# The samples' attention: own-maximum exponentials and value sums on VectorE, with shares and norm in small steps

## The chip, the core and the metric

One core of a Trainium2 chip runs the whole program. Its engines are TensorE (PE in the profile: matrix products, with PEld for the loading of the stationary operand), VectorE (DVE), ScalarE (ACT), GpSimd (POOL) and SyncE (SP), which issues most DMAs; each engine works through its own queue in order, and semaphores hold an instruction until its inputs are there. TensorE writes its results to PSUM (8 banks here, four in the pool `pmm` and four in `paux`), which DVE and ACT read; POOL does not touch PSUM in this kernel. The metric is the device time of one execution in microseconds, lower is better; the median of several runs is compared.

## The reference

One inference step of two layers, for a prompt of 256 tokens and for 8 samples of one token each, which share the weights. Each layer: a half-weighted SwiGLU, a mixer (a short gated convolution in layer 0, a gated linear recurrence in layer 1), cross attention to 256 memory rows, a second SwiGLU; a norm ahead of each. All is float32, and x has 1024 columns. The part that the change touches is the cross attention:

```python
def cross_attn(x, mk, mv, w_q, w_o):
    B, T, D = x.shape
    q = (x @ w_q).reshape(B, T, X_HEADS, X_HEAD_DIM)
    s = jnp.einsum('bthd,bnhd->bhtn', q, mk.astype(q.dtype)).astype(jnp.float32) / math.sqrt(X_HEAD_DIM)
    p = jax.nn.softmax(s, axis=-1).astype(x.dtype)
    o = jnp.einsum('bhtn,bnhd->bthd', p, mv.astype(x.dtype)).reshape(B, T, D)
    return o @ w_o
```

The prompt's keys and values (`mk`, `mv`) are products of the memory with `w_xkv`, made here; the 8 samples have keys and values of their own, read from a cache of 256 rows, 4 heads and 256 columns per sample and layer.

## The kernel before

**Layout.** x is held transposed (`xT`: 8 blocks of 128 columns of the model, each 264 wide: 256 prompt tokens and 8 samples), so each product serves prompt and samples at once. float32 products are made of three: each factor is split into a high part rounded to the fast product format and the rest (`xh`, `xl` of x; `wh`, `wl` of a weight), and `mm3` (L336 to L338) multiplies high x high, high x low, low x high.

**Weights** (class `Weights`). They come in halves of 4 blocks (512 KB) through six raw buffers, loaded on SP's queue (L96), rounded to `wh` on ACT (L107) and split to `wl` on DVE or POOL, as `W.lo` says (L122: "v" or "p"). `advance()` does one split, one rounding and the loads that fit, once per `flow.tick()`; a half can be rounded once a buffer out of five is free (`first_live` marks the first half still in use). `W.after` names an instruction behind which later roundings or splits on an engine have to stand, and `order(a, b)` puts a behind b in an engine's queue.

**Flow.** Work beside the main products is written as generators in three lanes; each `flow.tick()` between products advances every lane by one step up to its next `yield`. A planner then orders each engine's queue: by and large in the order of issue, but an instruction whose inputs it takes to be ready can run ahead of its step; `tc.high_priority(offset=HURRY)` moves some forward.

**Norms** (class `Norm`). For each block of x that is finished, `high`, `low` and `square` make `xh` (ACT), `xl` (DVE, L361) and add the square to `acc` (ACT, then POOL, L373). After the last block, `finish` waits three steps, splits `acc` (`nhi` on ACT, `nlo` on DVE, L383), and one step later makes the factor R from a product with ones, Ln and Exp on ACT and three dependent DVE steps (L324 to L330). The next projection runs on unscaled x meanwhile; R is first needed when its results leave PSUM (`evac_q`, L952, for the queries).

**Attention of one layer** (`attention`). `project` makes the queries of the four heads (tile `qT`), two heads first side by side in 8 steps. In lane 1 `mem_split` makes `mh` (ACT, L943) and `ml` (DVE, L944) of the memory. `do_kv(h)` makes keys and values of the prompt for one head: 8 blocks of 6 products of 512 columns (L966 to L968, tile `kv`), with a tick after each; then lane 1 follows with `transpose_k` (`pkt`, `KTt`), `prompt_scores` (`psc`, softmax, `ppt`) and `prompt_values` (`po`, into `oh` and `ol`). `project_late` is the output projection: it runs over blocks 0 to 5 for three chunks (two first, then the third) before the last head of the prompt is complete, and then ends.

**The samples** run in lane 0. `sample_scores(h)` lays each sample's query on 16 partitions and multiplies and adds with 16 key rows per partition on DVE (L1020, two instructions a row), four rows per step; partition 16b+g holds rows of sample b. After all four heads `sample_rest` takes the maximum over heads and partitions through two small products (`pst`), the exponentials for all heads, a third small product for the sums, multiplies shares into `Ps` (L1108, one column per sample) and makes 64 products of 8 rows and 256 columns with the value rows (L1122, tile `spv`, four heads beside each other in the array), four value rows of all heads per step, then a copy, two transposes (`spt`), and the last 8 columns of `oh` and `ol`. Key and value rows come through `Ring`: four buffers of 1 MB, filled on SP's queue in the order of the line (8 of keys, 8 of values per layer, then the state tiles for the recurrence), each as soon as `ring.done` gives a buffer back. `W.lo` is "p" from the end of `project` until the samples are drained, just ahead of `project_late`.

## Time and profile before

| | |
|---|---|
| median of 3 runs | 1293.19 us (1293.01 to 1293.26) |
| the profiled execution | 1294.13 us |
| its span, first to last instruction | 1292.3 us |
| mean granted TensorE clock | 0.998 |
| HBM read / written | 259.19 MB / 10.10 MB |

The profile is of one execution. Its page gives each engine's busy time, 40 slices of the span, the DMA queues, the chain of work that ended last, and the costliest groups of instructions; the trace also answers by stretch of time, by tile, by line and by wait. "core: us, PE busy (x) ..." rows give, per stretch, length, busy time and count of each engine, the granted clock, the mean share of the 16 DMA engines that was busy, and the rate in GB/s. In rows of groups, out<-in is followed by the shapes, the count, then busy us and mean ns of one, then idle time ahead of it and who ended it. In rows in order of time, the first number is the start and the second the length, in us; brackets hold idle time and its releaser. A matmul's listed duration is its passage through the array; several are under way at once.

### The profile page before, as it was taken

The page shows a single profiled execution, that of the slowest core. Times are in us where ns is not written, and L with a number is a line of the kernel's source. Part 1 is how long each engine was busy: PE and PEld are TensorE (multiplying, and loading weights), DVE is VectorE, ACT ScalarE, POOL GpSimd, SP SyncE. Part 2 cuts the span into 40 slices and gives each one's busy share as a digit, 9 for nine tenths or more (in the row PEclk, how much of TensorE's full clock was granted, in tenths as well). Part 3 has the DMA queues.
Part 4 walks back from the last instruction along what each step waited for, and adds up shares of the span by engine and source line. Part 5 has one row for each costly group of instructions (what it writes and reads, how often), then busy time and mean ns, then how long its engine had stood idle before and what let it go on. Part 6 is the DMA issues. An engine that isn't in the chain of part 4 may idle for free.

```text
span 1292.3 us, 25856 instructions
## 1 busy us (share of the span) xinstructions
PE 1271.4 (98%) x10267; PEld 1233.7 (95%) x10267; DVE 826.4 (64%) x1561; ACT 692.4 (54%) x1131; POOL 292.1 (23%) x236
## 2 busy tenths in 40 slices
PE   8999999999999999999999999999999999999996
PEld 8999999999869999999999999999998789999996
DVE  7655567759925755546655545887888728766454
ACT  6455545446545655544645544656575446766542
POOL 2211231212650211132111132000013531112220
PEclk9999999999999999999999999999999999999999
DMA  8796555646998666556666656563547995997550
GB/s 274 239 304 178 167 180 183 197 148 196 352 372 255 185 176 191 172 165 193 191 181 179 183 168 193 175 189 114 189 149 238 393 359 151 292 315 236 167 164 35
DMA packets 263755, 270.98 MB, mean 210 GB/s; under 512 B 8777, under 2 KB 259721, under 8 KB 261074
## 3 DMA queue, kind: packets, MB, share of 16 engines
q1 hardware_dynamic: 257726, 263.98, 64.9%
q10 hardware_dynamic: 5908, 5.35, 1.2%
q8 instruction: 81, 1.33, 0.4%
q14 instruction: 40, 0.33, 0.1%
HBM read 259.19 MB, written 10.10 MB: 208 GB/s over the span
## 4 chain that ended last, share of the span: by engine, by line
PE 92%; DVE 4%; ACT 1%; issue 1%; DMA 1%; POOL 0%; SPq 0%; DVEq 0%; ACTq 0%; POOLq 0%
PE pj L336 19%; PE pj L337 19%; PE pj L338 19%; PE dn L336 7%; PE dn L338 7%; PE dn L337 7%; PE kv L967 2%; PE kv L966 2%; PE kv L968 2%; DVE xl L361 2%; DVE wl L122 1%; PE spv L1122 1%; PE psc L1048 1%; PE pj L414 1%; PE pl L1288 1%
## 5 line engine op out<-in xcount | busy, mean ns | idle before, releaser
L122 DVE TENSOR_TENSOR wl<-raw,wh 128x1024 fp32r<-128x1024 f32 (+1 forms) x348 | 426.7, 1232 | 240.4 <-ACT wh L107 228.1
L336 PE MATMUL pj<-xh,wh 128*128 128x264 f32 x1952 | 558.4, 286 | 5.0 <-DVE qT L952 2.5
L337 PE MATMUL pj<-xl,wh 128*128 128x264 f32 x1952 | 553.4, 284 | 0.0
L338 PE MATMUL pj<-xh,wl 128*128 128x264 f32 x1952 | 553.0, 283 | 0.0
L107 ACT CAST wh<-raw 128x1024 fp32r<-128x1024 f32 (+1 forms) x406 | 415.9, 1032 | 255.5 <-PE pj L337 121.5
L336 PEld LDWEIGHTS pj<-xh,wh 128*128 128x128 f32 x1952 | 367.8, 188 | 7.3 <-DVE qT L952 3.0
L337 PEld LDWEIGHTS pj<-xl,wh 128*128 128x128 f32 x1952 | 368.0, 189 | 0.0
L338 PEld LDWEIGHTS pj<-xh,wl 128*128 128x128 f32 x1952 | 366.2, 188 | 0.0
L336 PE MATMUL dn<-ah,wh 128*128 128x264 f32 x704 | 200.9, 285 | 0.0
L338 PE MATMUL dn<-ah,wl 128*128 128x264 f32 x704 | 200.0, 284 | 0.0
L337 PE MATMUL dn<-al,wh 128*128 128x264 f32 x704 | 199.4, 283 | 0.0
L816 POOL TENSOR_TENSOR al<-a,ah 128x264 fp32r<-128x264 f32 x88 | 90.4, 1029 | 411.8 <-ACT ah L815 411.6
L122 POOL TENSOR_TENSOR wl<-raw,wh 128x1024 fp32r<-128x1024 f32 (+1 forms) x60 | 140.5, 2351 | 186.1 <-ACT wh L107 119.9
L338 PEld LDWEIGHTS dn<-ah,wl 128*128 128x128 f32 x704 | 132.7, 188 | 0.0
L336 PEld LDWEIGHTS dn<-ah,wh 128*128 128x128 f32 x704 | 132.4, 188 | 0.2
L337 PEld LDWEIGHTS dn<-al,wh 128*128 128x128 f32 x704 | 132.5, 188 | 0.0
L312 ACT ACTIVATE g<-g 128x264 f32<-128x264 f32 x88 | 36.9, 424 | 76.3 <-DVE g L808 76.3
L815 ACT CAST ah<-a 128x264 fp32r<-128x264 f32 x88 | 36.0, 413 | 69.0 <-DVE a L814 68.9
L356 ACT ACTIVATE xh<-xT,gains 128x264 fp32r<-128x264 f32 x56 | 28.2, 513 | 74.2 <-DVE xT L842 59.1
L1020 DVE CUSTOM_DVE_ANT_0 junk<-ring,pq 128x256 f32<-128x256 f32 x128 | 53.7, 419 | 3.7
L808 DVE TENSOR_TENSOR g<-pj,R_norm_ffn 128x264 f32<-128x264 f32 x88 | 37.5, 430 | 28.5 <-PE pj L338 28.2
L814 DVE TENSOR_TENSOR a<-g,pj 128x264 f32<-128x264 f32 x88 | 37.1, 426 | 26.2 <-PE pj L338 25.2
(325 smaller groups left out, 1481.3 us busy)
## 6 DMA issues: line engine op xcount, KB each, us to landing
raw<-in_w_ffn_gate_dram SPq DMA_DIRECT2D x88, 512.0 KB, 5.6
raw<-in_w_ffn_up_dram SPq DMA_DIRECT2D x88, 512.0 KB, 3.8
raw<-in_w_ffn_down_dram SPq DMA_DIRECT2D x64, 512.0 KB, 3.4
ring<-in_cache_mem_k_dram SPq DMA_DIRECT2D x16, 1024.0 KB, 7.7
raw<-in_w_xkv_dram SPq DMA_DIRECT2D x64, 256.0 KB, 4.8
ring<-in_cache_mem_v_dram SPq DMA_DIRECT2D x16, 1024.0 KB, 8.7
raw<-in_w_rec_in_dram SPq DMA_DIRECT2D x32, 512.0 KB, 4.2
raw<-in_w_ffn_down_dram SPq DMA_DIRECT2D x32, 384.0 KB, 2.9
```

What stands on the lines that cost most here:

```text
L107: ins = self.behind(self.hi[i % len(self.hi)], copy(wh[:, :n], self.raw[i][:, :n]))
L122: ins = eng.tensor_sub(wl[:, :n], self.raw.pop(i)[:, :n], wh[:, :n].bitcast(F32))
L312: in_line(nc.scalar.activation(dst, src, func, **kw))
L336: nc.tensor.matmul(ps, wh[:, s], rh, start=first, stop=False)
L337: nc.tensor.matmul(ps, wh[:, s], rl, start=False, stop=False)
L338: nc.tensor.matmul(ps, wl[:, s], rh, start=False, stop=last)
L356: W.pin(nc.scalar.activation(xh[:, k, :n], src, AF.Copy, scale=gcol(self.name, self.layer, k)))
L808: nc.vector.tensor_mul(g, ps, norm.R)
L814: nc.vector.tensor_mul(a, g, ps)
L815: nc.scalar.copy(ah[:, blk], a)
L816: nc.gpsimd.tensor_sub(al[:, blk], a, ah[:, blk].bitcast(F32))
L1020: nc.vector.tensor_tensor_reduce(junk, t[:, i % 8], pq[:, :XD], 1.0, 0.0, ALU.mult, ALU.add, sc[:, h, i : i + 1])
```

## The change

Per layer, the diff does this:

- `sample_scores`: five key rows per step instead of four; when a head's 16 scores are there, each partition takes its own negative maximum and its own exponentials and their sum. The queries leave PSUM already divided by 16.
- `sample_rest`: after five idle steps, DVE sums the value rows for a pair of heads at a time, weighted with the unscaled exponentials: 16 rows x 2 heads, two rows per step, in a PSUM bank (`acc`); the last row goes to `total` in SBUF. Between the rows of the first pair, `combine` makes, one small piece per step, the common maximum, the correction factor of each partition, the common sum, and `oz`: the share factor, laid out per sample. Per pair, four products of `total` with `oz` (8 columns) then give the samples' output already transposed. The maxima, corrections and products are ordered behind the big product issued last (`flow.passed`).
- The value rows come as four rows of two heads per buffer, no longer two rows of four heads.
- Nothing drains the samples ahead of the output projection. `project_late` needs the first pair before block 0 and the second before block 4, and goes over blocks 0 to 3 of all three chunks before it goes to blocks 4 and 5.
- DVE to other engines: the memory's low part (`ml`) and the prompt's `vl` go to POOL (with one more copy on ACT for `ml`), the keys' copy `KTt` and the softmax's scaling go to ACT. `W.lo` is "p" from the seventh step of `mem_split` until the second pair is done.
- `Norm.finish`: ahead of the attention (`early`) the split of `acc` comes one step earlier, and in the step before the factor no weights are split or rounded (`held`); for the norm behind the attention, `xl` of the last four blocks is made behind the split of `acc`.

```diff
+SLACK = 5
+STEPS = (3, 5, 7, 9, 11, 13)
+LAG = 2
...
 
     def advance(self):
         n = len(self.halves)
-        if self.n_split < self.n_round:
+        if not self.held and self.n_split < self.n_round:
             self._split()
-        if self.n_round < n and self.n_round - self.first_live < W_BUFS:
+        if not self.held and self.n_round < n and self.n_round - self.first_live < W_BUFS:
             self._round()
...
         def finish(self):
-            yield
-            yield
-            yield
+            for _ in range(3 - self.early):
+                yield
             hi, lo = (cp.tile([P, NC], F32R, tag="nsq", name=n, bufs=2) for n in ("nhi", "nlo"))
-            nc.scalar.copy(hi, self.acc)
-            nc.vector.tensor_sub(lo, self.acc, hi.bitcast(F32))
-            yield
+            into = nc.scalar.copy(hi, self.acc)
+            rest = nc.vector.tensor_sub(lo, self.acc, hi.bitcast(F32))
+            if self.early or self.lows:
+                W.after["s"], W.after["v"] = into.ins, rest.ins
+            for k in self.lows:
+                W.behind("v", self.low(k))
+            for n in range(1 + self.early):
+                W.held = self.early and n == 1
+                yield
+            W.held = False
             ps = aux_bank("ps_ms")
...
+        for a, b in ((0, HK), (HK, k0)):
+            need(a)
+            for k in range(a, b):
+                for c in range(2):
+                    block(c, k)
+                if k == HK - 1:
+                    W.first_live = first[0] + 2
                 flow.tick()
+            for k in range(a, b):
+                block(2, k)
+                if k == HK - 1:
+                    W.first_live = first[1]
+                if k % 2:
+                    flow.tick()
         ready()
...
-        def fill_v(i2):
+        def fill_v(pair, i4):
             def f(t):
                 rows = ins["cache_mem_v"][l].rearrange("b (g i) h d -> (b g) i (h d)", i=NI)
-                nc.sync.dma_start(t.rearrange("p (i e) -> p i e", i=2), rows[:, 2 * i2 : 2 * i2 + 2])
+                at = slice(2 * pair * XD, 2 * pair * XD + 2 * XD)
+                nc.sync.dma_start(t.rearrange("p (i e) -> p i e", i=4), rows[:, 4 * i4 : 4 * i4 + 4, at])
 
             return f
...
+        if late is not None:
+            nxt.lows = range(KT - 4, KT)
...
+                    nxt.low(k - 1)
+            nxt.kt(k, low=k != KT - 2 if late is None else k not in nxt.lows)
...
                     yield
+                W.lo = ("p",)
                 for k in range(KT):
                     g = gcol("norm_mem", l, k)
-                    nc.scalar.activation(mh[:, k], memT[:, k], AF.Copy, scale=g)
-                    nc.vector.scalar_tensor_tensor(
-                        ml[:, k], memT[:, k], g, mh[:, k].bitcast(F32), op0=ALU.mult, op1=ALU.subtract
-                    )
+                    mg = ap.tile([P, NMEM], F32, tag="mg", name=f"mg{k}", bufs=2)
+                    W.behind("s", nc.scalar.activation(mg, memT[:, k], AF.Copy, scale=g))
+                    nc.scalar.copy(mh[:, k], mg)
+                    nc.gpsimd.tensor_sub(ml[:, k], mg, mh[:, k].bitcast(F32))
                     yield
 
-                nc.vector.tensor_mul(qTs[h][:, j], ps, norm.R)
+                nc.vector.scalar_tensor_tensor(qTs[h][:, j], ps, 1.0 / 16.0, norm.R, op0=ALU.mult, op1=ALU.mult)
...
-                nc.vector.tensor_sub(vl, vn, vh.bitcast(F32))
+                nc.gpsimd.tensor_sub(vl, vn, vh.bitcast(F32))
...
-                nc.vector.tensor_copy(KTt[h], pt.rearrange("p (t n) -> p t n", t=2))
+                nc.scalar.copy(KTt[h], pt.rearrange("p (t n) -> p t n", t=2))
...
-                    if i % 4 == 3:
+                    if i % 5 == 4:
                         yield
+                nc.vector.reduce_max(mx[:, h : h + 1], sc[:, h], axis=AX.X, negate=True)
+                act(sc[:, h], sc[:, h], AF.Exp, bias=mx[:, h : h + 1], accum_out=zs[:, h : h + 1])
...
-                    nc.vector.tensor_scalar(pr[:, r], pr[:, r], zs[:, r : r + 1], None, op0=ALU.mult)
+                    nc.scalar.activation(pr[:, r], pr[:, r], AF.Copy, scale=zs[:, r : r + 1])
...
+            def combine():
+                pt = aux_bank("pst")
+                order(nc.tensor.transpose(pt[:XH, :P], mx, ident), flow.passed, "products in line")
+                yield
+                top, f, g = pt[:XH, 2 * P : 2 * P + NB], pt[:, P + 2 * XH : P + 3 * XH], pt[:, P + 3 * XH : P + 4 * XH]
+                nc.vector.tensor_reduce(top, pt[:XH, :P].rearrange("h (b g) -> h b g", b=NB), axis=AX.X, op=ALU.min)
+                nc.vector.tensor_copy(tops[:XH].rearrange("h (b g) -> h b g", b=NB), spread(top))
+                yield
+                order(
+                    nc.tensor.matmul(pt[:, P : P + XH], tops, ident[:, :XH], start=True, stop=True),
+                    flow.passed,
+                    "products in line",
+                )
+                nc.vector.tensor_sub(mx, pt[:, P : P + XH], mx)
+                act(f, mx, AF.Exp)
+                yield
+                nc.vector.tensor_mul(zs, zs, f)
+                yield
+                order(
+                    nc.tensor.matmul(pt[:, P + XH : P + 2 * XH], peers, zs, start=True, stop=True),
+                    flow.passed,
+                    "products in line",
+                )
+                yield
+                nc.vector.reciprocal(rz, pt[:, P + XH : P + 2 * XH])
+                nc.vector.tensor_mul(g, rz, f)
+                nc.vector.tensor_mul(
+                    oz, g.unsqueeze(2).broadcast_to([P, XH, NB]), own.unsqueeze(1).broadcast_to([P, XH, NB])
+                )
             def sample_rest():
...
+                for _ in range(SLACK):
+                    yield
+                steps = combine()
+                for pair in range(XH // 2):
+                    acc = aux_bank("acc")
+                    total = ap.tile([P, 2, XD], F32, tag="total", name="total", bufs=1)
+                    for i in range(NI):
+                        t = ring.tiles[l, "v", pair, i // 4].rearrange("p (i h d) -> p i h d", i=4, h=2)
+                        for j in range(2):
+                            p, sums = sc[:, 2 * pair + j, i : i + 1], acc[:, j * XD : j * XD + XD]
+                            if i == 0:
+                                nc.vector.tensor_scalar(sums, t[:, i % 4, j], p, None, op0=ALU.mult)
+                            else:
+                                dst = total[:, j] if i == NI - 1 else sums
+                                nc.vector.scalar_tensor_tensor(
+                                    dst, t[:, i % 4, j], p, sums, op0=ALU.mult, op1=ALU.add
+                                )
+                        if i % 4 == 3:
+                            ring.done((l, "v", pair, i // 4))
+                        if pair == 0 and i in STEPS:
+                            next(steps, None)
+                        if i % 2:
+                            yield
+                    for _ in range(LAG):
+                        yield
+                    pt = aux_bank("spt")
+                    for j in range(2):
+                        for dt in range(2):
+                            o = pt[:, (2 * j + dt) * NB : (2 * j + dt) * NB + NB]
+                            d = slice(dt * P, dt * P + P)
+                            order(
+                                nc.tensor.matmul(o, total[:, j, d], oz[:, 2 * pair + j], start=True, stop=True),
+                                flow.passed,
+                                "products in line",
                             )
+                    with tc.high_priority(offset=HURRY):
+                        ptv = pt[:, : 4 * NB].rearrange("p (t b) -> p t b", b=NB)
+                        ohv, olv = (t[:, 4 * pair : 4 * pair + 4, T:] for t in (oh, ol))
+                        nc.scalar.copy(ohv, ptv)
+                        nc.vector.tensor_sub(olv, ptv, ohv.bitcast(F32))
+                    sampled.add(pair)
                     yield
+
+            def until(pair):
+                while pair not in sampled:
+                    flow.step()
+                if pair:
+                    W.lo = ("v",)
 
             flow.spawn(1, mem_split())
             project(XH, xh, xl, evac_q, need=norm)
-            W.lo = ("p",)
             for h in range(XH):
                 do_kv(h)
-            flow.drain(0)
-            W.lo = ("v",)
-            out_proj(oh, ol, nxt, late=(KT - 2, lambda: flow.drain(1)))
+            out_proj(oh, ol, nxt, late=(KT - 2, lambda k: until(k // 4), lambda: flow.drain(1)))
```

`mm3` now returns its last product, which `flow.passed` keeps. Of the old `sample_rest` only the removed lines are left out above; they stand in the print of the kernel (L1087 to L1141).

More of the change, by code (lines that the diff above doesn't have):

```diff
@@ L769, in add_cache @@
                 ring.add((l, "k", h, hf), fill_k(h, hf))
-        for i2 in range(NI // 2):
-            ring.add((l, "v", i2), fill_v(i2))
+        for pair in range(XH // 2):
+            for i4 in range(NI // 4):
+                ring.add((l, "v", pair, i4), fill_v(pair, i4))
     def add_states(key):
@@ L1132, in sample_rest @@
-                for h in range(XH):
-                    nc.scalar.copy(os[32 * h : 32 * h + NB], ps[32 * h : 32 * h + NB, :XD])
-                yield
-                pt = aux_bank("spt")
-                for dt in range(2):
-                    nc.tensor.transpose(pt[:, dt * P : dt * P + P], os[:, dt * P : dt * P + P], ident)
-                ptv = pt[:, : 2 * P].rearrange("p (t h r) -> p h t r", t=2, r=32)[:, :, :, :NB]
-                ohv, olv = (t[:, :, T:].rearrange("p (h t) b -> p h t b", t=2) for t in (oh, ol))
```

86 lines of the change are left out of this document (19 added, 67 removed).

## The prediction

> **What bounds the kernel now.** I read the page's busy shares first, then TensorE's waits, then the attention stage in both layers by stretches, then the chain of waits inside it, and last the rows of each operation that the change moves. The program computes attention twice, with the same schedule: 315 to 392 us in layer 0 and 979 to 1056 us in layer 1.
>
> ```profile
> PE 1271.4 (98%) x10267; PEld 1233.7 (95%) x10267; DVE 826.4 (64%) x1561; ACT 692.4 (54%) x1131; POOL 292.1 (23%) x236
> PE pj L336 <- DVE qT L952: 2.5, 2, 1.5
> PE pj L336 <- DVE xT L850: 2.4, 2, 1.2
> ...
> core 0: us, PE busy (x) PEld busy (x) DVE busy (x) ACT busy (x) POOL busy (x), PEclk, DMA share, GB/s
> 979.00:1056.00 77.00, 76.80 (x502) 61.55 (x503) 47.13 (x170) 36.41 (x67) 40.73 (x17) 1.00 1.00 351
> ...
> 315.20:392.00 76.80, 76.57 (x499) 61.25 (x500) 46.82 (x170) 36.28 (x66) 40.76 (x17) 1.00 1.01 347
> 392.00:400.70 8.70, 8.70 (x66) 8.30 (x64) 5.43 (x10) 4.39 (x10) 0.00 (x0) 1.00 1.14 340
> ```
>
> TensorE is busy 98% of the span, at full granted clock (PEclk 1.00), and in the attention stretch it idles 0.2 us of 77. So an instruction taken off TensorE is worth its full issue time, and anything added to DVE (VectorE), ACT or POOL is free until TensorE waits for it. DVE has 30 us idle in 76.8, POOL 36, ACT 40. The DMA share is not free at all: 1.0.
>
> **The change, part by part: TensorE.** The samples' 64 value products per layer (spv; 128 records each layer, 256 in all) go, and so do their two transposes (spt). Pieces of the chain of waits show what a group holds up:
>
> ```profile
> L1122 PE MATMUL spv<-ring,Ps 128*8 128x256 f32 x256 | 15.3, 379 | 0.0
> L1137 PE MATMUL spt<-ident,os 128*128 128x128 f32 x4 | 0.9, 300 | 0.1
> ...
> 361.00 0.12 PE pst L1105 x2
> ...
> 362.82 1.84 PE spv L1122 x32
> 364.66 0.43 PE kv L966
> 365.09 0.23 PE kv L967
> ...
> 369.68 0.44 PE ppt L1062 x4
> ...
> 388.29 0.44 PE spt L1137 x2
> ...
> 1048.50 1.84 PE spv L1122 x32
> ```
>
> The 379 ns of one record is its passage, not its cost: 32 records take 1.84 us, and the product behind takes 0.43 in place of 0.23. First and last group agree at 1.84. Eight groups of 1.84 + 0.20 are **16.3 us**; two pairs of transposes at 0.44 are 0.9. Removed: 17.2.
>
> Added are 16 products with a 128x128 stationary tile and 8 columns, two records each. The nearest row is pst L1105 (4 columns, two records): 0.12. Above it stands the 128-column transpose, 0.44/4 = 0.11 a record, so 0.22 a product. So 1.9 to 3.5 us, and 0.2 behind each of the four groups, 0.8. I take the lower, since the columns are few: **2.7 added** (end 4.3). The three small share products stay, only spread out. TensorE's work: -14.5, at worst -12.9.
>
> **The two stalls around the stage.** TensorE's waits of 2.5 and 2.4 us are four gaps, two per layer. In layer 0:
>
> ```profile
> 307.88 3.25 DVE L944 SCALAR_TENSOR_TENSOR ml<-memT,gains,mh 128x256 fp32r<-128x256 f32 x8
> 311.20 0.43 DVE L324 SCALAR_TENSOR_TENSOR nacc_norm_xattn<-ps_ms,R_norm_xattn 128x264 f32<-128x264 f32 x1
> 311.67 0.43 DVE L328 SCALAR_TENSOR_TENSOR nacc_norm_xattn<-nacc_norm_xattn,R_norm_xattn 128x264 f32<-128x264 f32 x1
> 312.13 0.43 DVE L330 SCALAR_TENSOR_TENSOR R_norm_xattn<-nacc_norm_xattn,R_norm_xattn 128x264 f32<-128x264 f32 x1
> 312.48 2.35 DVE L122 TENSOR_TENSOR wl<-raw,wh 128x1024 fp32r<-128x1024 f32 x2
> 314.75 1.45 DVE L952 TENSOR_TENSOR qT<-pj,R_norm_xattn 128x264 f32<-128x264 f32 x4
> ...
> 315.23 0.39 PE L336 MATMUL pj<-xh,wh 128*128 128x264 f32 x1 [1.00 <-DVE qT L952]
> ...
> 422.59 2.79 DVE L361 SCALAR_TENSOR_TENSOR xl<-xT,gains,xh 128x264 fp32r<-128x264 f32 x3
> 425.30 0.42 DVE L850 TENSOR_TENSOR xT<-xT,pj 128x264 f32<-128x264 f32 x1
> ...
> 425.77 0.39 PE L336 MATMUL pj<-xh,wh 128*128 128x264 f32 x1 [1.22 <-DVE xT L850]
> ```
>
> At 315 the queries' evacuation qT frees a PSUM bank for TensorE, and it stands behind two weight splits (2.35 us) that stand behind the norm's factor. The change holds splits back for one step ahead of that factor and moves the eight ml off DVE: qT could start near 312.6, before TensorE needs it. At 425.8 the last addition into xT stands behind three xl (2.79 us); the change sends the last four xl behind the squares. What is late next is xl of block 4, needed nine steps of 0.73 us (six products of 0.12) after the restart: 6.5 us, against some 2 us for four xl; covered. Of 4.9 us I take **4.0** as gone (ends 0 and 4.9).
>
> **What DVE takes on.** 64 sums a layer, each 256 wide: one input in SBUF (V row), one in PSUM (the sum), a scalar per partition in SBUF, result to PSUM. No row of DVE writes PSUM, so this price is bounded:
>
> ```profile
> 11.03 4.76 POOL L122 TENSOR_TENSOR wl<-raw,wh 128x1024 fp32r<-128x1024 f32 x2 [9.73 <-DVE wh L107]
> ...
> 10.86 2.44 DVE L361 SCALAR_TENSOR_TENSOR xl<-px,gains,xh 128x256 fp32r<-128x256 f32 x6
> ...
> L361 DVE SCALAR_TENSOR_TENSOR xl<-xT,gains,xh x56: 482/574/1053, 159.4 to 1090.4; 128x264 fp32r<-128x264 f32 x56
> L361 DVE SCALAR_TENSOR_TENSOR xl<-px,gains,xh x8: 474/476/478, 9.4 to 12.8; 128x256 fp32r<-128x256 f32 x8
> ```
>
> Nearest is xl<-px: same instruction, width, PSUM and SBUF inputs and scalar, result to SBUF: six in 2.44 us, (2.44 - 0.476)/5 = 0.39 from start to start. The upper end is a sum that waits for the one before: the norm's dependent steps start 0.47 apart with 0.43 each, so 0.476 + 0.04 = 0.52. I take 0.39 (the two heads of a pair alternate, so no sum reads its neighbour's result): 25.2 us a layer, 33.3 at the upper end. A PSUM write dearer than that is a rival below. Off DVE go:
>
> ```profile
> L122 DVE TENSOR_TENSOR wl<-raw,wh 128x1024 fp32r<-128x1024 f32 x4 | 4.8, 1220 | 0.0
> ...
> L1040 DVE TENSOR_SCALAR Pp<-Pp,zsp 128x256 f32<-128x256 f32 x4 | 2.3, 628 | 0.0
> ...
> L984 DVE TENSOR_TENSOR Vl<-Vn,Vh 128x512 fp32r<-128x512 f32 x3 | 2.1, 689 | 3.3 <-ACT Vh L983 3.3
> L1000 DVE COPY KTt<-pkt 128x512 f32<-128x512 f32 x3 | 2.1, 685 | 0.6 <-PE pkt L996 0.6
> ...
> L1108 DVE SCALAR_TENSOR_TENSOR Ps<-sc,rzs,own 128x128 f32<-128x128 f32 x4 | 1.1, 348 | 0.1
> ```
>
> The sums must end where the output projection first needs heads 2 and 3, which the new order puts behind its first 12 blocks, 12 x 0.73 = 8.7 us. From 315.2 to there DVE worked 46.8 + 5.4 = 52.3 us; less 12.4 (the five rows), plus 25.2, it needs 65.1. TensorE gives 85.5 - 8.6 = 76.9. So DVE has **11.8 us to spare** a layer, 3.7 at 0.52 each. The sums follow the scores only by five steps, but DVE runs what is ready ahead of its step: the eight ml above, written one per step from the seventh on, ran in a row before the norm's factor.
>
> **POOL and ACT.** POOL's price for a split and for narrower subtractions:
>
> ```profile
> L122 POOL TENSOR_TENSOR wl<-raw,wh 128x1024 fp32r<-128x1024 f32 x54 | 129.4, 2408 | 169.4 <-ACT wh L107 103.2 <-DMA raw<-in_w_xkv_dram 44.9 <-DVE wh L107 9.7
> ...
> L122 POOL TENSOR_TENSOR wl<-raw,wh 128x768 fp32r<-128x768 f32 x6 | 11.1, 1846 | 16.7 <-ACT wh L107 16.7
> ...
> L373 POOL TENSOR_TENSOR nacc_norm_mix<-nacc_norm_mix,nsq 128x264 f32<-128x264 f32 x14 | 10.6, 757 | 51.3 <-ACT nsq L372 51.3
> ```
>
> POOL keeps its 17 splits (40.8 us), takes over the four of DVE's row and about one of the output projection (5 x 2.41 = 12.0), eight ml at some 0.76 (6.1), three vl, an estimate of 1.3 between the 264 and 768 wide rows (3.9): 62.8 of 76.9 us. It fits, but is tightest at the start of the keys' and values' products, where ml, splits and the first halves meet. ACT gains three key copies, six scalings and eight copies of half a microsecond, some 8 us on 41, with half its time free. **Queues behind the new waits.** On TensorE the share products and the transposing products wait for small DVE steps that were issued one or two steps earlier; behind them in TensorE's order stand the keys' and values' products, so each microsecond that DVE lags beyond those steps is lost. On SP's queue a V load now waits for DVE's sums instead of spv, and the weight loads stand behind it; six raw buffers, 2.9 us of products each (24 of 0.12), cover some 17 us. V's bytes stay 8 MB a layer, in pieces of 2 KB instead of 8; the key loads, in pieces of 1 KB, are part of the stretch that moves 367 GB/s (quoted below), so I cost the pieces at nothing; without that cover the price is the transfers' rival. On POOL, ACT, the share products' place in DVE's queue, and the PSUM banks that the running sum now holds, I charge **2.0 us of new waits** for both layers (ends 0 and 8, 4 us a layer being what is left when 0.52 takes the slack).
>
> **Sum.** -14.5 - 4.0 + 2.0 = -16.5 against the profiled execution's own 1294.1 (span 1292.3 and 1.8 around it): 1277.6. The median of the runs, 1293.2, is 0.9 below it, so the forecast is **1276.7**. With every good end, -14.5 - 4.9 = -19.4, 1273.8; with every bad one, -12.9 + 8 = -4.9, 1288.3.
>
> **Rivals.**
> *The sums' price (DVE late).* At 0.52 or a little more, or with bunching in the queue, the slack of 11.8 falls below 4 and TensorE waits some 4 us a layer at heads 2 and 3: 1276.7 + 8 - 2 = 1283. Against it: the xl<-px row. For it: nothing here writes PSUM from DVE.
>
> *The transfers are the bound.* For it:
>
> ```profile
> DMA packets 19580, 23.69 MB, mean 367 GB/s; under 512 B 694, under 2 KB 18551, under 8 KB 18551
> ...
> ring<-in_state_rec_dram SPq DMA_DIRECT2D x8, 512.0 KB, 5.4
> ```
>
> From 327.4 to 392, 23.69 MB moved in 64.6 us with the engines full. If all of it had to move before the products end, the stage could not shrink by 8.6: 14.5 us of work taken off would come back as waits, with 4 - 2 left: 1291. Against it: eight state loads, 8 x 512 KB = 4.2 MB, are prefetches for a later stage, and the new ring frees their buffers only as DVE ends pair 1. 19.5 MB at 367 GB/s is 53.1 us, and 56.0 are there. The margin is 3 us, and the same queue carries the weights, so a part of this may come.
>
> *Slower: POOL stops the sums.* xl<-xT, with both tensors in SBUF, takes 482 at least and up to 1053 ns; if the sums were shut out while POOL works, POOL's 62.8 and DVE's 65.1 would no longer lie beside each other. Only the sums' share counts: in some 45 us of theirs POOL holds 62.8 x 45/76.9 = 37, so 25.2 + 37 - 45 = 17 us are late per layer, less the 11.8 to spare elsewhere at best: 5 to 17, so 1287 to 1311; taken at 12, 1301. It turns slower from 1293.2, 8 us lost a layer. Against it: xl<-px, one tensor in SBUF and one in PSUM, ran at 474 to 478 while POOL's 4.76 us of splits ran. The page "SBUF — State Buffer" of the Trainium skill, section "Who interferes with whom", says that a DVE instruction with two SBUF inputs is fully blocked by a GpSimd one that reads SBUF, and one with at most one is not; the two rows agree, but it does not say whether the scalar counts, which only xl<-px shows. By the blocked reading the sum would be the 1301 of this rival.
>
> *The change does little of what it says.* The waits at qT and xT reappear behind other work, and the new products wait on DVE: 1294.1 - 14.5 + 6 - 0.9 = 1285, near the first rival; counted with it.
>
> **How the numbers follow.** Forecast (1273.8 to 1281) 0.60; DVE late 0.20; transfers 0.09; POOL stops the sums, or DVE's PSUM write costs over 0.72 (25.2 + 11.8 + 8.3 lost = 45.3 over 64, the same bound) 0.07; a gain beyond 1273.8, 0.04. The range of 8 in 10 runs from 1272.5, just past the good end, to 1287.5, the bad end less the transfers' case. A measurement here tells about 0.2%, 2.6 us: faster is below 1290.6. Faster gets 0.60 + 0.20 + 0.04 and a third of the transfers' case, 0.87; the rest of that case, 0.06, is same; slower 0.07.
>
> **What would show it.** No spv rows; 128 sums on DVE at starts 0.39 to 0.52 apart; no gap before TensorE's pj behind qT and xT; the attention stretch 8 us shorter per layer. A TensorE wait on the sum tile (total), on oz or ol would show the first rival; on wh or wl behind raw, the transfers; sums of 0.7 us and more beside POOL's splits, the third. The prediction is wrong if TensorE waits over 4 us a layer on any of these.

## The result and the profile after

The changed kernel took **1279.76 us** (median of 4 runs, 1279.03 to 1282.15), the kernel before 1293.22: a ratio of 0.9899, 95% interval 0.9882 to 0.9917, or 13.5 us less. The forecast was 1276.7. The profiled execution is the slowest of the four, 1282.15 us with a span of 1280.4, so its sums are made against the profiled 1294.13 of before: 12.0 us less.

The page of the changed kernel, engines' busy time; then TensorE's waits (engine, line, whom it waited for: total us, times, longest):

```profile
PE 1258.7 (98%) x10039; PEld 1230.7 (96%) x10039; DVE 842.4 (66%) x1625; ACT 703.4 (55%) x1167; POOL 346.9 (27%) x272
```

```profile
PE ppt L1084 <- ACT Pp L1062: 3.6, 2, 2.3
...
PE pj L340 <- DVE ol L1181: 1.4, 2, 0.7
...
PE pj L339 <- ACT oh L1180: 0.5, 2, 0.3
PE ps_ms L398 <- DVE nlo L387: 0.4, 2, 0.2
PE psc L1070 <- ACT KTt L1021: 0.3, 1, 0.3
```

TensorE's busy time fell by 12.7 us, and both old gaps, behind qT and behind xT ahead of the next projection, are gone. In their place stand 6.2 us of new ones, and the largest, 3.6, is at a place that the prediction didn't name: ppt, the transposes of the prompt's softmax, waits for ScalarE's scaled shares (`Pp`).

The samples' sums on DVE, by tile (line, count: shortest/median/longest ns, first and last start); then a piece of the chain of work in the second layer (start, us until the next piece):

```profile
L1156 DVE SCALAR_TENSOR_TENSOR acc<-ring,sc,acc x112: 467/490/491, 355.4 to 1054.3; 128x256 f32<-128x256 f32 x112
...
L1156 DVE SCALAR_TENSOR_TENSOR total<-ring,sc,acc x8: 472/480/484, 376.8 to 1055.2; 128x256 f32<-128x256 f32 x8
```

```profile
1036.20 0.79 PE spt L1173 x8
1036.99 0.33 PE kv L987
```

No sum takes longer than 491 ns, whether POOL works or not. The eight records (four products) of spt hold TensorE for 0.79 us, and the product behind them starts 0.10 late: four groups at 0.89 are 3.6 us, where 2.7 was forecast.

The gain is uneven. The next projection's first product on unscaled x, in order of time, of the kernel before and of the changed one (first layer, then second):

```profile
421.78 0.28 PE L336 MATMUL pj<-xh,wh 128*128 128x264 f32 x1
...
1085.45 0.28 PE L336 MATMUL pj<-xh,wh 128*128 128x264 f32 x1
```

```profile
417.87 0.28 PE L339 MATMUL pj<-xh,wh 128*128 128x264 f32 x1
...
1074.26 0.28 PE L339 MATMUL pj<-xh,wh 128*128 128x264 f32 x1
```

3.9 us were won by the end of the first layer's attention and 11.2 by the end of the second's. So the first layer loses some 3 us that the second does not. TensorE's row in order of time, and the stretches around it (length, PE busy, ..., then PEclk, the granted clock), show where:

```profile
349.98 1.30 PE L1084 MATMUL ppt<-ident,Pp 128*128 128x128 f32 x4 [2.33 <-ACT Pp L1062]
350.93 0.78 PE L987 MATMUL kv<-wh,mh 128*128 128x512 f32 x1
...
353.51 0.40 PE L987 MATMUL kv<-wh,mh 128*128 128x512 f32 x1
```

```profile
348.00:350.00 2.00, 0.02 (x1) 0.02 (x1) 1.90 (x10) 2.00 (x7) 0.40 (x1) 0.98 1.09 390
350.00:351.00 1.00, 1.00 (x5) 0.79 (x5) 0.93 (x5) 0.84 (x2) 1.00 (x1) 0.50 1.05 403
...
352.00:353.00 1.00, 1.00 (x4) 0.81 (x3) 0.99 (x5) 0.01 (x1) 1.00 (x1) 0.50 1.06 385
353.00:354.00 1.00, 1.00 (x5) 0.76 (x5) 0.67 (x5) 0.00 (x0) 1.00 (x1) 0.83 1.08 397
```

TensorE stood for 2.33 us and then ran at half the granted clock for more than 3. The four transposes held it for 0.95 us (349.98 to 350.93) where the prediction's chain row has 0.44, and the next six products took from 350.93 to 353.51, 2.6 us in place of 6 x 0.23: 1.7 us more in all, and with the wait 4.0 at one place. In the second profile of this kernel, below, the same ten products behind a wait of 1.61 us took 2.17 us at full clock, against 3.53 here (349.98 to 353.51): so some 1.4 of the 1.7 are the half clock, and the rest came without it. In the second layer the same wait is 1.3 us, and the clock stays at 1.00 behind it.

Back from there. TensorE's row of the prompt's scores and DVE's rows, in order of time, show why Pp is late, and SP's waits between 300 and 345 us why DVE is:

```profile
341.52 1.99 PE L1070 MATMUL psc<-KTt,qT 128*128 128x256 f32 x8 [0.35 <-ACT KTt L1021]
```

```profile
345.11 0.42 DVE L1043 CUSTOM_DVE_ANT_0 junk<-ring,pq 128x256 f32<-128x256 f32 x1 [2.19 <-DMA ring<-in_cache_mem_k_dram]
...
346.85 0.69 DVE L1057 TENSOR_REDUCE mxp<-psc 128x2 f32<-128x512 f32 x1
```

```profile
SPq L99 <- POOL wl L125: 14.3, 6, 5.3
SPq L99 <- DVE wl L125: 8.7, 6, 3.3
```

The prompt's scores psc were ready at 343.5, but their maximum mxp stands in DVE's queue behind samples' scores that wait for a key load. SP, which issues key loads and weight loads from one queue, had stood 14.3 us for POOL's splits, whose ends free the raw weight buffers. Such waits are not new, but they grew: with DVE's splits they are 23.0 us here, and were 18.3 in the kernel before (12.0 for DVE's, 6.3 for POOL's). The first key load issued in this stretch went out at 327.21 us, in the kernel before at 324.78. Of Pp's lateness another 0.5 us is ScalarE's: its scaling could start at 348.87, when the reciprocal ends, but stood behind a weight rounding until 349.41. POOL's rows in order of time:

```profile
315.15 4.76 POOL L125 TENSOR_TENSOR wl<-raw,wh 128x1024 fp32r<-128x1024 f32 x2 [0.21 <-DMA raw<-in_w_xkv_dram]
319.87 1.44 POOL L967 TENSOR_TENSOR ml<-mg,mh 128x256 fp32r<-128x256 f32 x2
...
323.79 4.79 POOL L125 TENSOR_TENSOR wl<-raw,wh 128x1024 fp32r<-128x1024 f32 x2
```

`W.lo = "p"` now starts at the seventh step of `mem_split`, so the first splits take 2.4 us each on POOL, with the ml between them, where DVE took 1.2. The DMA engines' busy tenths from 310 to 355 us, in 40 slices, say the same (changed kernel, then before; MB below each):

```profile
DMA  0199800194930004989989999999999999999999
...
DMA packets 11473, 12.07 MB, mean 268 GB/s; under 512 B 467, under 2 KB 10717, under 8 KB 11471
```

```profile
DMA  7000687898917869999999999999999999999999
...
DMA packets 12011, 13.58 MB, mean 302 GB/s; under 512 B 542, under 2 KB 11757, under 8 KB 11757
```

The changed kernel moved 1.5 MB less by 355 us, ahead of a stretch in which the DMA engines are full.

### The profile page after: what moved, and what is told of

Its sections match the earlier page's. It is cut to its first block, busy times and chain, and to the rows that moved or that the text cites. A ratio compares the mean times of both kernels' runs of the same rounds, so it can differ in the third digit from the quotient of the medians.

```text
span 1280.4 us, 25535 instructions
## 1 busy us (share of the span) xinstructions
PE 1258.7 (98%) x10039; PEld 1230.7 (96%) x10039; DVE 842.4 (66%) x1625; ACT 703.4 (55%) x1167; POOL 346.9 (27%) x272
## 4 chain that ended last, share of the span: by engine, by line
PE 91%; DVE 3%; ACT 2%; DMA 2%; POOL 1%; issue 1%; SPq 0%; DVEq 0%; POOLq 0%; ACTq 0%
PE pj L340 20%; PE pj L339 20%; PE pj L341 20%; PE dn L339 7%; PE dn L341 7%; PE dn L340 7%; PE kv L987 2%; PE kv L988 2%; PE kv L989 2%; ACT wh L110 1%; DVE wl L125 1%; PE pl L1333 1%; PE psc L1070 1%; DMA ring<-in_cache_mem_k_dram 1%; DVE xl L365 1%; DMA raw<-in_w_xkv_dram 1%
## 5 line engine op out<-in xcount | busy, mean ns | idle before, releaser
L125 DVE TENSOR_TENSOR wl<-raw,wh 128x1024 fp32r<-128x1024 f32 (+1 forms) x334 | 411.7, 1238 | 240.0 <-ACT wh L110 224.2
L125 POOL TENSOR_TENSOR wl<-raw,wh 128x1024 fp32r<-128x1024 f32 (+1 forms) x74 | 173.3, 2356 | 127.2 <-ACT wh L110 108.3
L378 POOL TENSOR_TENSOR nacc_norm_xattn<-nacc_norm_xattn,nsq 128x264 f32<-128x264 f32 x14 | 13.6, 972 | 174.8 <-ACT nsq L377 174.5
L1156 DVE SCALAR_TENSOR_TENSOR acc<-ring,sc,acc 128x256 f32<-128x256 f32 x112 | 54.5, 487 | 2.7
```

The source lines that it names most:

```text
L125: ins = eng.tensor_sub(wl[:, :n], self.raw.pop(i)[:, :n], wh[:, :n].bitcast(F32))
L1156: nc.vector.scalar_tensor_tensor(dst, t[:, i % 4, j], p, sums, op0=ALU.mult, op1=ALU.add)
```

## The experiments

**The theory**: early splits on POOL hold raw buffers, SP's queue holds the key loads behind the weight loads, DVE's scores and the prompt's maximum come late, TensorE waits at ppt. **Rivals**: the ppt wait is a matter of DVE's order alone; DVE is simply too full with sums; the transfers are the bound.

### The changed kernel again

The same kernel on the chip of the next three experiments, with nothing edited.

> The changed kernel again, beside the experiments on the same chip: 1279 to 1282 us by every theory. If TensorE's wait for Pp (2.3 us in layer 0) and the half clock behind it belong to the slow one of the four runs only, this profile shows a shorter wait and some 1279.5; if they are in every run, the wait is there again.

Measured: 1282.35 us (1281.02 to 1283.68), ratio 0.9915 (0.990 to 0.993). Here the ppt waits are 3.0 us, the longer one 1.61, and the clock stays at 1.00 behind it. The two medians of the same kernel are 2.6 us apart (the chip of the first is not on record); the next three are held against 1282.35.

### POOL's splits begin after the queries

```diff
             def mem_split():
                 for _ in range(6):
                     yield
-                W.lo = ("p",)
...
             project(XH, xh, xl, evac_q, need=norm)
+            W.lo = ("p",)
```

The ml stay on POOL.

> POOL takes the weight splits only from the end of the queries' projection on, as in the kernel before; the rest of the change stays. Theory (raw buffers come free late behind POOL's splits, so SP's queue stands, the DMA engines idle from 310 to 326 us, and the key loads come late): SP waits for POOL's splits fall from 14 to under 7 us there, DVE's waits for key loads from 4.8 and 3.8 us to under 2 each, TensorE's wait for Pp goes, and the time is 3 to 5 us lower, 1275 to 1277. Rival (plain bandwidth of the transfers): the waits for key loads stay, time within 1 us of the changed kernel. Rival (DVE is the bound): DVE gets four splits of 1.2 us per layer back, 1 to 4 us slower.

Measured: **1277.22 us** (1277.10 to 1277.33), ratio 0.9875 (0.986 to 0.989). TensorE's waits here, from the largest in the attention on; then SP's waits between 300 and 345 us:

```profile
PE pj L340 <- DVE ol L1180: 1.4, 2, 0.7
...
PE pkt L1016 <- ACT Kn L996: 0.8, 2, 0.4
...
PE pj L339 <- ACT oh L1179: 0.5, 2, 0.3
```

```profile
SPq L99 <- DVE wl L125: 10.7, 6, 3.4
...
SPq L99 <- POOL wl L125: 1.0, 2, 0.8
```

POOL's 14.3 us on SP's queue became 1.0; DVE's splits, which come back, hold it for 10.7, so both together fell from 23.0 to 11.7 us. The first key load of the stretch goes out at 324.36, 13.16 MB have moved by 355 us, no score on DVE waits for a key load, and ppt doesn't wait. One line moved gives 5.1 us on the same chip (2.5 against the first median of the changed kernel). This version beats both kernels measured there, by 16.1 and by 5.1 us.

### The prompt's maximum ahead in DVE's queue

```diff
-                nc.vector.reduce_max(mx, src, axis=AX.X, negate=True)
+                with tc.high_priority(offset=HURRY):
+                    nc.vector.reduce_max(mx, src, axis=AX.X, negate=True)
```

The exponentials and the reciprocal are in the block too.

> The prompt's maximum, exponentials and reciprocal are moved forward in their queues, past scores that may wait for a key load. Theory (the maximum stands behind scores that wait for a load): TensorE's wait for Pp (3.6 us over both layers) and the half clock behind it go although DVE's waits for key loads stay, 3 to 5 us lower: 1275 to 1277. Rival (Pp is late through its scaling on ACT): the wait stays, time within 1 us.

Measured: 1281.97 us (1280.45 to 1284.38), ratio 0.9908 (0.9891 to 0.9924): no change, and the ppt waits are 3.6 us, as in the first profile of the changed kernel. The planner's priority did not bring the maximum ahead of scores that come late: it runs at 346.10 here, behind scores again, and psc was ready at 343.0. A miss for what I expected; it shows that this priority is no cure, not that the order is without effect.

### Two rows of sixteen

Value rows 1 to 14 are left out of the sums, so DVE has 56 fewer operations per layer; the loads stay.

```diff
-                            else:
-                                dst = total[:, j] if i == NI - 1 else sums
+                            elif i == NI - 1:
+                                dst = total[:, j]
```

> Leaves out the value rows 1 to 14 of the samples' sums, so 112 of the 128 sums in both layers are not made: DVE works some 29 us less per layer. Theory (the sums are hidden beside TensorE even at 0.52 us each): within 1.5 us of the changed kernel, and the wait for Pp stays. Rival (DVE late through the sums): the waits for ol and oh go and the time falls by 3 us or more.

Measured: 1286.76 us (1285.63 to 1289.36), ratio 0.9952 (0.9937 to 0.9967): less work on DVE, and 4.4 us slower, which neither reading expected. DVE's and TensorE's largest new waits:

```profile
DVE total L1156 <- DMA ring<-in_cache_mem_v_dram: 9.5, 2, 4.8
```

```profile
PE pst L1129 <- DVE zss L1126: 5.3, 2, 2.7
```

Without the sums between them, `total` reaches its value row before the load does and blocks DVE for 4.8 us, and the shares' small steps behind it keep TensorE. So this is no clean test of DVE's load. It shows that a queue in order pays for an instruction that stands too early, and that the ppt waits (2.8 us here) don't come from the number of sums. The changed kernel's own rows say so too: its first ppt wait ends at 349.98, and its first sum starts at 355.4.

### The running sum in SBUF

On the version with the late splits. This run and the three behind it were made on another chip, where the kernel before took 1293.11 us, against 1293.36 beside the runs above:

```diff
-                    acc = aux_bank("acc")
+                    acc = ap.tile([P, 2 * XD], F32, tag="acc", name="acc", bufs=1)
```

> This is e1_lo_late with one change: the running sums of the value rows lie in SBUF in place of a PSUM bank. Measured against e1_lo_late's 1277.2 us. Theory: 0.525 us from start to start is the price of writing the sum to PSUM; with the sum in SBUF a lone row of them starts every 0.40 us (as xl<-px did), but beside POOL's splits, with both tensors in SBUF, single sums take up to 1.05 us (as xl<-xT did). DVE gains 64 x 0.12 = 8 us a layer where POOL rests and loses where it works; TensorE has no wait on the sums in e1_lo_late, so the time moves by -1 to +6 us: 1276 to 1283. Rival 1: 0.525 is the price of two sums that alternate on one ring buffer, whatever they write: starts stay at 0.52 and the time at 1277. Rival 2 (the prediction's third case, POOL stops the sums, put to the test by making it so): sums beside POOL are slow throughout, 1287 or more.

Measured: 1310.44 us (1309.21 to 1311.14), ratio 1.0133 (1.0118 to 1.0148): 17 us slower than before, 33 slower than with the sum in PSUM, where I had expected -1 to +6. The sums by tile, then DVE's and POOL's rows in order of time:

```profile
L1155 DVE SCALAR_TENSOR_TENSOR acc<-ring,sc,acc x112: 450/472/2616, 353.1 to 1077.3; 128x256 f32<-128x256 f32 x112
```

```profile
365.30 1.26 DVE L1155 SCALAR_TENSOR_TENSOR acc<-ring,sc,acc 128x256 f32<-128x256 f32 x3
...
367.41 5.48 DVE L1155 SCALAR_TENSOR_TENSOR acc<-ring,sc,acc 128x256 f32<-128x256 f32 x3
```

```profile
367.44 5.17 POOL L125 TENSOR_TENSOR wl<-raw,wh 128x1024 fp32r<-128x1024 f32 x2 [4.13 <-ACT wh L110]
```

Two readings. With POOL idle, three sums take 1.26 us, so they start (1.26 - 0.47)/2 = 0.40 apart: the 0.52 of the changed kernel is the price of the sum in PSUM, and of its writing: the two `total` sums of a pair read the sum in PSUM too but write to SBUF, and in the version with the late splits they start 0.40 apart. Beside POOL's splits three sums take 5.48 us for two splits' 5.17: POOL shuts them out. That is the prediction's slower rival made real by one edit; its estimate was 1287 to 1311, taken at 1301. Of the 33 us, 19.5 are more idle time of TensorE, and its products ran for 23.6 us in stretches of half clock, where about half of the time is lost. The section "Who interferes with whom" of the Trainium skill's page "SBUF — State Buffer" says that a DVE instruction with two SBUF inputs contends with a GpSimd one that reads SBUF, and the rows agree, with 5.48 beside 5.17. With one tensor and the scalar in SBUF and the sum in PSUM, no sum exceeded 491 ns, so the scalar doesn't count.

### The key loads on ScalarE's queue

On the changed kernel:

```diff
-                nc.sync.dma_start(t.rearrange("p (i d) -> p i d", d=XD), rows[:, 8 * hf : 8 * hf + 8, h])
+                nc.scalar.dma_start(t.rearrange("p (i d) -> p i d", d=XD), rows[:, 8 * hf : 8 * hf + 8, h])
```

> This is the changed kernel with one change: the samples' key loads are issued from ACT's queue and no longer stand in SP's queue behind the weight loads. Theory (the key loads come late because SP waits for POOL's early splits): the scores' waits of 4.8 and 3.8 us for key loads go, and with them TensorE's waits of 3.6 us at ppt for Pp; the weight loads still wait for POOL. Time 1277 to 1279 against 1280 to 1282. Rival 1 (the late splits themselves cost the time, the key loads are a side effect): SP still waits 14 us for POOL, ppt still waits 2 us and more, time stays at 1280 to 1282. Rival 2 (ACT's queue is worse): an issue on ACT waits for a ring buffer that DVE frees, and ACT's exponentials and copies stand behind it: TensorE waits more, 1283 and up.

Measured: 1286.37 us (1285.11 to 1288.01), ratio 0.9952 (0.9935 to 0.9969). DVE waits for no key load, as the theory has it, and ppt waits once, 1.1 us, though SP still stands 15.0 us for POOL between 300 and 345 us: so it is the late key loads, and not the late weights, that had held most of ppt. But the second rival came: an issue on ACT stands for a ring buffer, and the casts behind it stand too. ACT's row in order of time:

```profile
333.61 1.05 ACT L110 CAST wh<-raw 128x1024 fp32r<-128x1024 f32 x1 [5.81 <-DVE sc L1043]
```

TensorE now waits 2.2 us at psc for ACT's key copy and 3.4 at spt for `total`, with 6.8 us of half clock behind the longest. What one queue gained, the queue that took over the issues lost, and more.

### One more operation per value row

On the version with the late splits; the added result goes unused:

```diff
+                            if j == 0:
+                                spare = ap.tile([P, XD], F32, tag="junk", name="spare", bufs=1)
+                                nc.vector.scalar_tensor_tensor(
+                                    spare, t[:, i % 4, j], p, sums, op0=ALU.mult, op1=ALU.add
+                                )
```

> This is e1_lo_late with one more operation of a sum's kind for every value row of every pair, 32 a layer, whose result goes unused to SBUF; the output is as before. A dose for the prediction's slack on DVE. 32 of 0.40 to 0.53 us are 13 to 17 us of DVE a layer. Theory 1 (from the profile of e1_lo_late: DVE is busy 37 of the 44 us in which keys' and values' products run, and the last sum ends just before its product on TensorE): only some 7 us are free there, so TensorE waits 6 to 10 us a layer on total or ol: 1289 to 1297. Theory 2 (the prediction's count over the whole stage, 11.8 us of slack at 0.39 a sum): since the sums measure 0.525, 3.7 us are left, and TensorE waits 9 to 13 us a layer: 1295 to 1303. Rival (DVE is not near a bound; the scheduler moves other work off the sums' way): 2 us a layer or less, 1277 to 1281.

Measured: 1319.51 us (1317.80 to 1320.36), ratio 1.0202 (1.0187 to 1.0218): 42 us for a dose of 32 x 0.52 = 16.6 us a layer, more than either theory gave. TensorE's waits, and the longer one of the first layer in order of time:

```profile
PE spt L1177 <- DVE total L1155: 34.5, 4, 16.5
```

```profile
414.51 1.85 PE L1177 MATMUL spt<-oz,total 128*128 128x8 f32 x8 [15.11 <-DVE total L1155]
```

All of the dose lands on TensorE (34.5 us of waits for 33.3 us of dose). The rest is half clock: behind the four waits TensorE works for 3.4, 4.6, 3.4 and 7.1 us at 0.50, 18.5 in all, of which half, 9.3, is lost. With the 1.9 us at ol and oh that go, 34.5 + 9.3 - 1.9 = 41.9, against 42.1 between the two profiled executions. So with the late splits DVE has no slack left at the end of the second pair. DVE's and TensorE's rows of that version say it too:

```profile
394.89 0.87 DVE L1155 SCALAR_TENSOR_TENSOR total<-ring,sc,acc 128x256 f32<-128x256 f32 x2
```

```profile
395.92 0.96 PE L1172 MATMUL spt<-oz,total 128*128 128x8 f32 x8
```

The last sum ends at 395.76, and TensorE comes to its product at 395.92, with no wait listed.

### The norm's edits taken out, and alone

First the version with the late splits, with `finish`, `low` and the last four xl as in the kernel before:

> This is e1_lo_late without the change's edits to the norm (no early step, splits not held, the last four xl in their old places). Theory: the old stalls return, 2 x 1.0 to 1.5 at qT and 2 x 1.22 at the last addition into xT, 4.9 us in all, and nothing else changes: 1277.2 + 4.9 = 1282.1, with TensorE's waits on DVE qT and DVE xT back at about 2.5 each. Rival 1: the eight ml's move to POOL alone had already freed qT, so only the 2.4 at xT return: 1279.6. Rival 2: the edits did not matter in the new order, 1277.

Measured: 1282.68 us (1282.48 to 1284.74), ratio 0.9923 (0.9908 to 0.9938), 5.5 us over the version with them. TensorE's waits:

```profile
PE pj L339 <- DVE xT L859: 2.5, 2, 1.2
PE pkt L1005 <- ACT Kn L985: 2.3, 4, 0.8
```

Then the kernel before with these edits alone:

```diff
-        self.order, self.after = None, {}
+        self.order, self.after, self.held = None, {}, False
...
+            for k in self.lows:
+                W.behind("v", self.low(k))
+            for n in range(1 + self.early):
+                W.held = self.early and n == 1
+                yield
+            W.held = False
```

> This is the kernel before with the change's edits to the norm alone (one step earlier, splits held behind it, the last four xl behind the squares). The samples' sums, the order of the value rows and POOL's and ACT's new work are not in it. Theory A (the prediction's: these edits free both stalls): all four gaps of the kernel before, 4.9 us, go: about 1288.4. Theory B (from e8_no_norm, where the gap at qT stayed away without them, since the eight ml were on POOL): the two gaps at xT (2.4 us) go, and qT's (2.5) stay or shrink, since the eight ml still run on DVE ahead of the norm's factor: 1289.5 to 1291. Rival (holding the splits makes others late): TensorE waits on wh or wl instead, 1292 or more.

Measured: 1290.26 us (1289.98 to 1290.39), ratio 0.9978 (0.9969 to 0.9987); the kernel before took 1293.01 beside it. The wait at qT, and DVE's rows ahead of it in order of time:

```profile
PE pj L336 <- DVE qT L964: 1.7, 2, 0.9
```

```profile
306.84 3.24 DVE L956 SCALAR_TENSOR_TENSOR ml<-memT,gains,mh 128x256 fp32r<-128x256 f32 x8
...
311.28 2.35 DVE L122 TENSOR_TENSOR wl<-raw,wh 128x1024 fp32r<-128x1024 f32 x2
313.55 1.44 DVE L964 TENSOR_TENSOR qT<-pj,R_norm_xattn 128x264 f32<-128x264 f32 x4
```

The two runs split the stalls. The xT gaps (2.4 us) go with the norm's edits and come back without them. The qT gap stays away without the norm's edits as long as the ml are on POOL, and shrinks only from 2.5 to 1.7 with them while the ml are on DVE: 3.24 us of ml ahead of the factor are its main cause. DVE's first step of the factor, at 311.20 in the kernel before, starts at 308.49 with the ml moved alone and at 308.35 in the changed kernel. The two splits still stand between the factor and qT, so `held` did not take them away. The first run's time fell on the expected 1282.1 by luck: the gap at qT, half of what was expected, did not come. Of its 5.5 us, 2.5 are xT, 1.5 pkt, and 1.1 are two waits at pq (0.6 and 0.5) that the version with the edits doesn't list; why pkt and pq wait was not isolated.

## Why the prediction held, and where it was off

The time lies in the forecast's own range; 3.1 us are missing to its middle. Step by step:

- **TensorE's work, -14.5.** Right. It can be read off the version with the late splits: 16.1 us gained, 4.9 of them by stalls that went, 2.7 lost to new waits (ol 1.4, pkt 0.8, oh 0.5, ps_ms 0.4, less 0.4 at pst that the kernel before had), which leaves 13.9. TensorE's busy time gives nearly the same without any residue: 1271.4 us before, 1257.3 in that version, which has no half clock in the attention, so 14.1. The products of spt at 3.6 in place of 2.7 cover the difference.
- **The stalls, -4.0.** All 4.9 went, the upper end. The reason given for xT held in both runs; of the two reasons given for qT, the ml's move was enough by itself, and the norm's edits without it brought 0.8 of 2.5.
- **DVE's sums at 0.39.** Mis-sized. They start 0.52 apart, the upper end, because writing the sum to PSUM costs more than the SBUF row from which 0.39 was taken; 0.40 is right for SBUF. At 0.52 the prediction left 3.7 us a layer (its stage left out the added products, 1.35 us a layer, so by its own terms 1.3 more). The time did not suffer, but the dose shows that nothing is left at the end of the second pair: idle time of DVE counted over the whole stage was not time that the last sums could use. The first rival (DVE late) did not come: even the 0.7 us at ol in each layer is no late sum. DVE takes a weight split of 2.19 us, from 400.12 on in the changed kernel, ahead of ol, which starts at 402.23.
- **New waits, +2.0.** This is the term that failed. In the version with the late splits they are 2.7, close to it. In the changed kernel the profiled execution has 6.2, less the old 0.4, and 1.7 of half clock: 7.5 us. Its stated ends, 0 and 8, hold that, but they were set by DVE's slack, so that the total stayed inside the range is in part luck. The prediction counted POOL over the whole stage (62.8 of 76.9 us), called the beginning tightest, and priced that at part of 2.0. It looked at SP's queue only for V loads that wait for sums with weight loads behind them; the other direction decided: weight loads that wait for POOL, with key loads behind them.
- **The transfers as the bound.** Not in this form: TensorE waits for no weight load, and the version with the late splits lets the loads run in time by moving an issue, not a byte. The part that came is late issue, with a DMA queue that is then too full to catch up.
- **POOL stops the sums.** Didn't come, for the reason given (one tensor in SBUF, one in PSUM). With the sum in SBUF it comes at full size: 33 us, where the prediction had 24 over its forecast and counted no half clock. (Its bound of 0.72 us a sum is 45.3/64 = 0.71.)
- **Sum.** With the terms as measured, -13.9 - 4.9 + 7.5 = -11.3, against 12.0 in the profiled execution. The 0.7 is not settled; the profiled execution of before lay 0.9 above its median and has a wait of 1.1 us (pj behind wh, L414) that the changed kernel's has not, which may be it. The version in which the one wrong term is cured runs at 1277.2, 0.5 from the forecast.

## What to carry to other kernels

Count an engine's load for the first microseconds of a stage as well as for all of it, and follow what its late results free: here POOL's splits free raw buffers, a free buffer lets the DMA queue go on, and only then are the loads issued that another engine needs. When work moves to a slower engine, move it at the point where its buffers are no longer scarce; one line was worth 5 us on the same chip. Before an operation goes to DVE beside a busy POOL, choose where its inputs lie: a sum in PSUM cost 0.12 us more each and saved 33 us in all.

## What the hardware showed unexpectedly

- Nine single waits of TensorE between 2.14 and 3.06 us were seen in the attention (2.33 in the changed kernel, 2.14 with the maximum given priority), and each was followed by 3.41 us at a granted clock of 0.50, once by twice that. Single waits of 1.00 to 1.61 us (the kernel before, the changed kernel again, the version without the norm's edits) left it at 1.00. But 1.42 and 1.43 us with one more operation per row did not, and neither did 1.46 and 1.03 us, 1.3 us apart, with the sum in SBUF. The one wait that was priced cost nearly twice its length (2.33 + 1.7 above). The Trainium skill's page "TensorE: Matmul & The Clock Gate", in "Part 1: The HAM clock gate", puts the drop behind an idle window of some 3.4 us; these waits were shorter, and the measurement decides.
- What decides can be read from the traces in good part. In each trace the edges of the granted clock lie on a fixed grid of 3.41 us. In the eleven traces, between 30 and 1255 us, TensorE idled for 64% or more of a stretch of this grid 21 times, and half clock followed each time; never for 47 to 63%. Of the other stretches six were followed by half clock too (0 to 38% idle), and why stays open. So the place of a wait on the grid counts beside its length: of the 2.33 us in the changed kernel, 2.27 fell into one stretch, the first row below, while the 1.61 us of its second profile fell across two, idle for 22% and 28%, and left the clock alone. The rows give length, PE busy and count, ..., then PEclk:

```profile
346.51:349.92 3.41, 1.14 (x6) 0.60 (x4) 3.27 (x15) 2.35 (x7) 0.84 (x2) 1.00 1.09 381
349.92:353.33 3.41, 3.35 (x10) 2.66 (x11) 3.23 (x14) 1.93 (x4) 3.41 (x2) 0.50 1.06 399
```

- DVE operations of one shape started 0.52 us apart with the running sum in PSUM and 0.40 with it in SBUF (POOL idle), though one alone takes 0.49 and 0.47.
